# State-space set-up queued behind the weight parts, and four set-up steps per feature tile in the opening

## The chip, the cores and the metric

One core of a Trainium2 chip runs one launch. The metric is the device time of that launch in microseconds; the median over three runs is compared.

## The reference

Two layers of a hybrid encoder trunk on 256 tokens of width 1024, in float32. Cut to what matters here:

```
for l in range(2):
    sh1, sc1, g1, ... g3 = split(silu(c) @ mod_w[l] + mod_b[l], 9)
    h = rms_norm(x, ffn1_norm[l]) * (1 + sc1) + sh1
    x = x + 0.5 * g1 * ((silu(h @ w_gate) * (h @ w_up)) @ w_down)     # first FFN, inner width 2816
    h = rms_norm(x, mix_norm[l]) * (1 + sc2) + sh2
    x = x + g2 * (concat(norm(attention), norm(s5_mixer), norm(conv)) @ w_out)
    h = rms_norm(x, ffn2_norm[l]) * (1 + sc3) + sh3
    x = x + 0.5 * g3 * swiglu(h)                                       # second FFN
return rms_norm(x, final_norm)
```

The `s5_mixer` is a diagonal state-space model with 16 groups of 64 complex states. Before any token is seen, it needs numbers that depend on the parameters alone: `exp(dt*a)` and its powers, the input matrices times these powers, the output matrices times them, and so on. This is the set-up of which the change speaks. The convolution's weights are laid out in it as well.

## The kernel before

**Weights.** All weights come as units of 128 x 1024 float32 (0.5 MB) through one stream (`Stream`, lines 63 to 128). A unit is loaded by the sync queue (SP) into one of six raw buffers. A weight unit is then prepared: ScalarE rounds it to `hi` (line 100), VectorE takes the rest `lo = raw - hi` (line 102), and TensorE multiplies with both (lines 328 to 330). There are six `hi` and six `lo` buffers. A raw buffer is given back when its `lo` is done. Between the weight units lie modulation units: VectorE itself multiplies and sums them (`macc`, line 365, two operations per unit), and the buffer is given back after that. `done` (line 126) counts a used weight unit and prepares further ones, up to five ahead.

**First FFN of layer 0.** It has an opening (`start`, line 484) for the first three of eleven column blocks. Eight feature tiles go through it; for each the scale and shift are first summed out of `mod_w` (`mod_cols`, for two tiles at a time, called for the next pair at the odd tiles), which ends for each tile in `hfs` on ScalarE (line 520) and `xTl` on VectorE (line 522). Then the tile's weights are prepared (`weights`) and 18 products run. At the end of each tile two set-up steps are traced, queued behind the newest `xTl` and `hfs`. After the opening, `silu` and `h` (lines 757 and 759) and two transposes (line 768) follow for its three blocks. The eight other blocks have four gate/up units each (`gt`, line 721) and the down units behind (`down`, line 775), 54 weight units in all, with 48 modulation units mixed in.

**Set-up.** `ssm_small` (line 825) and `ssm_layer` (line 962) are Python generators; each `yield` ends a step. For layer 0 a generator chains `setup_cols2`, `ssm_small(0)` and `ssm_layer(0)`, 59 steps; for layer 1 the last two, 58 steps. `ssm_small` works on tiles of 16 to 128 columns. In `ssm_layer`, lines 1011 to 1019 build `W` and `O` with products (lines 1014 and 1016) and sums (line 1018) of 512 columns, lines 1028 to 1040 the powers `Ec` and `Es`, lines 1057 to 1091 `R`, the kernel `Km`, the convolution's `W4` and `Tp`. A hook (`stages`, line 1497) traces steps at ticks: one tick follows each gate/up unit and each down block. `SLOTS0 = (1, 37, 43)` spreads 43 steps over 37 ticks from tick 1 of layer 0's first FFN, `SLOTS1 = (1, 42, 58)` the 58 of layer 1 over 42 ticks of layer 0's second FFN. Steps left over are traced after the last tick.

**Order.** Every engine runs a fixed queue. A planner writes the queues before the launch: among the instructions that are ready by its own estimate it takes the one that was traced first, with some blocks raised in rank (`high_priority`). So a set-up operation whose inputs are there may be placed ahead of the weight part traced next to it. `issue_after(ins)` ties the instructions traced in its block, on the engine of `ins` alone, to a place behind `ins` in that queue; it adds no wait. `behind` (line 76) does so for several instructions. The steps at the ticks are in no such block.

Of the kernel before, what the change touches and what calls it, by code (L numbers as in the profile page):

```python
# [9 lines left out]
F32 = mybir.dt.float32  # L10
# [3 lines left out]
AF = mybir.ActivationFunctionType  # L14
# [12 lines left out]
ADG = (((0,),(1,),(2,3)),((0,1,2,3),))  # L27
HIP = 150
HIPT = 50
SLOTS0 = (1, 37, 43)  # L30
SSTART = 2
SLOTS1 = (1, 42, 58)
UW = 264
NEG_INADM = -3.0e38
NEG_TAKEN = -3.3e38
# [27 lines left out]
class Stream:  # L63


    def __init__(self, tc, raw_p, hl_p):
        self.tc, self.nc, self.raw_p, self.hl_p = tc, tc.nc, raw_p, hl_p
        self.after_hi = self.after_lo = ()
        self.units = []
        self.loaded = self.prepped = self.got = 0  # L70
        self.used = self.wprep = 0
        self.ready = []
        self.names = []
        self.hb = HB

    def behind(self, ins):
# [13 lines left out]
    def prep_one(self):  # L90
        nc = self.nc
        self.load_upto(self.prepped + RB)
        u = self.units[self.prepped]
        raw = u["raw"]
        if u["kind"] == "w":
            n = u["n"]
            hi = self.hl_p.tile([P, UN], F32R, tag="hi", name="hi")
            lo = self.hl_p.tile([P, UN], F32R, tag="lo", name="lo")
            with self.behind(self.after_hi):
                nc.scalar.activation(hi[:, :n], raw[:, :n], AF.Copy)  # L100
            with self.behind(self.after_lo):
                nc.vector.tensor_sub(lo[:, :n], raw[:, :n], hi[:, :n].bitcast(F32))  # L102
            self.ready.append((hi, lo))
            self.names.append(u.get("name"))
            self.wprep += 1
        else:
            with self.behind(self.after_lo):
                u["use"](raw)
        self.prepped += 1
        self.load_upto(self.prepped + RB)  # L110
# [21 lines left out]
def kernel(  # L132
# [8 lines left out]
    nc = tc.nc  # L141
# [25 lines left out]
    def b8(shape, nm):  # L167
        return two_p.tile(shape, F32, tag="b8", name=nm, bufs=2)
# [171 lines left out]
    st = Stream(tc, raw_p, hl_p)  # L340
# [64 lines left out]
    def unspill(l, m):  # L405

        r = rows[(l, m)] = row_p.tile([P, D], F32, tag="g", name=f"row{l}_{m}")
        nc.gpsimd.dma_start(r, spill[(l, m)][0].partition_broadcast(P))
# [75 lines left out]
    def start():  # L484
# [56 lines left out]
        for k in range(KD):  # L541
# [16 lines left out]
            with st.behind([xti[max(xti)], hfi[max(xti)]]):  # L558
                for _ in range(SSTART):
                    next(setup0, None)  # L560
# [534 lines left out]
    def mixer(l, finish):  # L1095
# [295 lines left out]
        def conv_thread():  # L1391
            for j in range(2):
# [4 lines left out]
                if j == 0:  # L1397
                    U4 = b8([P, 4, 2, UW], "U4")
                for a in range(4):
                    (nc.scalar if a % 2 else nc.gpsimd).dma_start(U4[32 * a:32 * a + 32, :, j], uT[:, j, 8 * a:8 * a + UW])  # L1400
                yield
# [91 lines left out]
    def chain(*gens):  # L1493
        for g_ in gens:
            yield from g_

    def stages(gen, first, n, steps):

        def hook(u):
            if first <= u < first + n:  # L1500
                i = u - first
                for _ in range((i + 1) * steps // n - i * steps // n):
                    next(gen, None)
            elif u >= first + n:
                for _ in gen:
                    pass
        return hook
# [21 lines left out]
    for l in range(L):  # L1529
        if l == 0:  # L1530
            h1 = stages(setup0, *SLOTS0)
        else:
# [16 lines left out]
        mixer(l, after_mix)  # L1549
        ffn(l, 6, after_ffn2, stages(chain(ssm_small(l + 1), ssm_layer(l + 1)), *SLOTS1) if l + 1 < L else None, lambda: unspill(l, 8))  # L1550

# [30 lines left out]
```

## Time and profile before

| what | value |
| --- | --- |
| median of three runs | 1156.27 us (1149.23 to 1161.38) |
| profiled execution | 1159.37 us, its span 1157.5 us |
| TensorE busy | 1082.1 us (93%) |
| VectorE busy | 881.8 us (76%) |
| ScalarE busy | 557.9 us (48%) |
| GpSimd busy | 93.2 us (8%) |
| loads and stores | 251.43 MB, mean 217 GB/s |
| `hi`, line 100 | 314 operations, 328.0 us, 1054 ns each |
| `lo`, line 102 | 314 operations, 379.1 us, 1214 ns each |
| `macc`, line 365 | 224 operations, 166.3 us, 749 ns each |

The span runs from the first to the last instruction of one profiled execution; the device time has a little around it. Busy time is the time in which an engine had an instruction of its own running; matmul ends are modelled, so a busy TensorE need not be at its peak. The granted clock is the share of 2.4 GHz that TensorE's clock had. The DMA share is the busy time of 16 DMA engines as a share of the stretch. In a timeline a bracket gives the idle time ahead of an instruction and what ended it.

### The profile page before, as it was taken

The page shows a single profiled execution, that of the slowest core. Times are in us where ns is not written, and L with a number is a line of the kernel's source. Part 1 is how long each engine was busy: PE and PEld are TensorE (multiplying, and loading weights), DVE is VectorE, ACT ScalarE, POOL GpSimd, SP SyncE. Part 2 cuts the span into 40 slices and gives each one's busy share as a digit, 9 for nine tenths or more (in the row PEclk, how much of TensorE's full clock was granted, in tenths as well). Part 3 has the DMA queues.
Part 4 walks back from the last instruction along what each step waited for, and adds up shares of the span by engine and source line. Part 5 has one row for each costly group of instructions (what it writes and reads, how often), then busy time and mean ns, then how long its engine had stood idle before and what let it go on. Part 6 is the DMA issues. An engine that isn't in the chain of part 4 may idle for free.

```text
span 1157.5 us, 19306 instructions
## 1 busy us (share of the span) xinstructions
PE 1082.1 (93%) x7043; PEld 936.8 (81%) x7043; DVE 881.8 (76%) x1791; ACT 557.9 (48%) x979; POOL 93.2 (8%) x176
## 2 busy tenths in 40 slices
PE   5999978998999999999998999999899998999996
PEld 3578867886886878888996799999698687999996
DVE  4479998888597687899856889889678777665655
ACT  4354433446436565563534534444464656444442
POOL 6000101021012000000020000100100000000000
PEclk9899999989797899999999999999999899999998
DMA  9889788996653139768873799999665234767651
GB/s 254 268 268 304 227 258 287 328 292 175 159 149 78 57 103 301 246 223 287 262 220 108 250 323 360 339 317 328 184 165 148 73 91 146 256 210 221 210 160 55
DMA packets 182671, 251.43 MB, mean 217 GB/s; under 512 B 20023, under 2 KB 132865, under 8 KB 182577
## 3 DMA queue, kind: packets, MB, share of 16 engines
q1 hardware_dynamic: 173728, 240.56, 65.3%
q0 software_dynamic: 5792, 7.52, 2.8%
q10 hardware_dynamic: 3056, 2.13, 0.9%
q8 instruction: 55, 0.90, 0.3%
q14 instruction: 40, 0.32, 0.1%
HBM read 245.19 MB, written 1.11 MB: 213 GB/s over the span
## 4 chain that ended last, share of the span: by engine, by line
PE 56%; DMA 7%; DVE 6%; ACT 3%; issue 2%; SPq 1%; ACTq 0%; DVEq 0%
PE ps_gt L328 7%; PE ps_gt L329 7%; PE ps_gt L330 7%; PE ps_y L330 5%; PE ps_y L328 5%; PE ps_y L329 5%; DMA raw<-in_mod_w_dram 3%; DMA raw<-in_ffn_w_gu_dram 2%; DVE lo L102 2%; DVE macc L365 2%; ACT hi L100 1%; PE ps_idx L1201 1%; PE ps_gu L328 1%; PE ps_gu L330 1%; PE ps_cv L1408 1%
## 5 line engine op out<-in xcount | busy, mean ns | idle before, releaser
L100 ACT ACTIVATE hi<-raw 128x1024 fp32r<-128x1024 f32 (+1 forms) x314 | 328.0, 1054 | 315.0 <-DMA raw<-in_ffn_w_gu_dram 105.5
L102 DVE TENSOR_TENSOR lo<-raw,hi 128x1024 fp32r<-128x1024 f32 (+1 forms) x314 | 379.1, 1214 | 121.6 <-ACT hi L100 117.6
L328 PE MATMUL ps_gt<-xTh,hi 128*128 128x256 f32 x1120 | 320.2, 288 | 10.4 <-DVE h L745 6.6
L330 PE MATMUL ps_gt<-xTh,lo 128*128 128x256 f32 x1120 | 314.8, 285 | 4.4 <-DVE lo L102 4.4
L329 PE MATMUL ps_gt<-xTl,hi 128*128 128x256 f32 x1120 | 317.7, 285 | 0.0
L328 PEld LDWEIGHTS ps_gt<-xTh,hi 128*128 128x128 f32 x1120 | 216.2, 193 | 17.4 <-DVE h L745 7.6
L330 PEld LDWEIGHTS ps_gt<-xTh,lo 128*128 128x128 f32 x1120 | 214.4, 193 | 6.2 <-DVE lo L102 5.7
L329 PEld LDWEIGHTS ps_gt<-xTl,hi 128*128 128x128 f32 x1120 | 216.7, 193 | 1.8 <-issue 0.8
L365 DVE SCALAR_TENSOR_TENSOR macc<-raw,cond,macc 128x512 f32<-128x512 f32 x224 | 166.3, 749 | 25.8 <-DMA raw<-in_mod_w_dram 24.3
L329 PE MATMUL ps_y<-lo,hTh 128*128 128x512 f32 x352 | 139.9, 397 | 1.5 <-DVE lo L102 1.5
L330 PE MATMUL ps_y<-hi,hTl 128*128 128x512 f32 x352 | 139.5, 396 | 1.0 <-DVE hTl L749 1.0
L328 PE MATMUL ps_y<-hi,hTh 128*128 128x512 f32 x352 | 133.6, 396 | 4.9 <-ACT hi L100 4.5
L397 POOL DMA_DIRECT2D spill<-mrow x64 | 31.3, 496 | 642.0 <-ACT mrow L394 640.5
L328 PEld LDWEIGHTS ps_y<-hi,hTh 128*128 128x128 f32 x352 | 66.0, 189 | 19.3 <-ACT hi L100 5.3
L330 PEld LDWEIGHTS ps_y<-hi,hTl 128*128 128x128 f32 x352 | 67.1, 191 | 17.1 <-DVE hTl L749 2.1
L329 PEld LDWEIGHTS ps_y<-lo,hTh 128*128 128x128 f32 x352 | 67.3, 191 | 16.3 <-DVE lo L102 3.6
L328 PE MATMUL ps_gu<-hi,xTh 128*128 128x512 f32 x96 | 39.8, 415 | 6.8 <-DVE xTh L324 6.8
L743 ACT ACTIVATE silu<-ps_gt 128x256 f32<-128x256 f32 x70 | 25.3, 378 | 40.8 <-PE ps_gt L330 40.7
L330 PE MATMUL ps_gu<-hi,xTl 128*128 128x512 f32 x96 | 39.7, 414 | 3.0 <-DVE xTl L325 3.0
L329 PE MATMUL ps_gu<-lo,xTh 128*128 128x512 f32 x96 | 38.6, 402 | 0.0
L745 DVE TENSOR_TENSOR h<-silu,ps_gt 128x256 f32<-128x256 f32 x70 | 28.0, 417 | 10.6 <-ACT silu L743 10.4
L748 ACT ACTIVATE hTh<-h 128x256 fp32r<-128x256 f32 x70 | 27.4, 410 | 16.6 <-DVE h L745 15.5
(386 smaller groups left out, 1591.5 us busy)
## 6 DMA issues: line engine op xcount, KB each, us to landing
raw<-in_ffn_w_gu_dram SPq DMA_DIRECT2D x140, 512.0 KB
raw<-in_mod_w_dram SPq DMA_DIRECT2D x128, 512.0 KB
raw<-in_ffn_w_down_dram SPq DMA_DIRECT2D x88, 512.0 KB
raw<-in_ffn_w_gu_dram SPq DMA_DIRECT2D x72, 256.0 KB
raw<-in_w_in_dram SPq DMA_DIRECT2D x20, 512.0 KB
raw<-in_mod_w_dram SPq DMA_DIRECT2D x32, 256.0 KB
raw<-in_w_out_dram SPq DMA_DIRECT2D x16, 512.0 KB
row<-spill POOLq DMA_DIRECT2D x6, 512.0 KB, 4.9
```

Source lines behind the costliest of these rows:

```text
L100: nc.scalar.activation(hi[:, :n], raw[:, :n], AF.Copy)
L102: nc.vector.tensor_sub(lo[:, :n], raw[:, :n], hi[:, :n].bitcast(F32))
L328: return [nc.tensor.matmul(ps, xh, wh, start=start, stop=False), nc.tensor.matmul(ps, xh, wl, start=False, stop=False), nc.tensor.matmul(p ...
L329: nc.tensor.matmul(ps, xh, wl, start=False, stop=False),
L330: nc.tensor.matmul(ps, xl, wh, start=False, stop=stop)]
L365: nc.vector.scalar_tensor_tensor(acc, raw[:, 512 * i:512 * i + 512], cond[:, k:k + 1], prev, op0=ALU.mult, op1=ALU.add)
L397: nc.gpsimd.dma_start(d[:, 256 * q:256 * q + 256], r[32 * q:32 * q + 1, 0:256])
L743: nc.scalar.activation(s, ps[i][:, :256], AF.Silu)
L745: nc.vector.tensor_mul(h, s, ps[i][:, 256:])
L748: nc.scalar.activation(hi, h, AF.Copy)
L1201: nc.tensor.matmul(ps[:, nk * i:nk * i + nk], qiT[32 * b:32 * b + 32, 256 * i + P * t:256 * i + P * t + P], kiT[32 * b:32 * b + 32, :nk], ...
L1408: nc.tensor.matmul(pc[32 * q:32 * q + 32, 256 * ct:256 * ct + 256], SS["W4"][:, 32 * ct + 8 * q + b, :], U4[:, q, ct, b:b + 256], start=(b ...
```

## The change

A weight unit's two preparing instructions are kept in a list. At each tick, in both FFNs that carry set-up, the steps are traced in a block that queues their ScalarE and VectorE instructions behind the `hi` and `lo` of the third-newest weight unit traced so far (two back from the newest). In the opening four steps are traced per feature tile, not two, 32 in all, and 27 are left for the ticks.

```
-SLOTS0 = (1, 37, 43)
-SSTART = 2
+SLOTS0 = (1, 37, 27)
+SSTART = 4
 SLOTS1 = (1, 42, 58)
+AHEAD = 2
...
+        self.parts = []
...
             with self.behind(self.after_hi):
-                nc.scalar.activation(hi[:, :n], raw[:, :n], AF.Copy)
+                ih = nc.scalar.activation(hi[:, :n], raw[:, :n], AF.Copy)
             with self.behind(self.after_lo):
-                nc.vector.tensor_sub(lo[:, :n], raw[:, :n], hi[:, :n].bitcast(F32))
+                il = nc.vector.tensor_sub(lo[:, :n], raw[:, :n], hi[:, :n].bitcast(F32))
+            self.parts.append((ih, il))
...
             if first <= u < first + n:
                 i = u - first
-                for _ in range((i + 1) * steps // n - i * steps // n):
-                    next(gen, None)
+
+                with st.behind(st.parts[-1 - AHEAD]):
+                    for _ in range((i + 1) * steps // n - i * steps // n):
+                        next(gen, None)
```

## Rows read from the trace of the kernel before

**Rows 1.** Busy time by stretch: length, busy us (count) per engine, TensorE clock, DMA share, GB/s.

```profile
80.00:120.00 40.00, 39.56 (x269) 36.09 (x270) 36.26 (x80) 20.17 (x37) 2.11 (x3) 1.00 0.91 306
120.00:200.00 80.00, 68.34 (x445) 59.43 (x444) 72.46 (x129) 28.90 (x49) 8.66 (x17) 0.96 0.79 254
200.00:260.00 60.00, 56.56 (x390) 50.95 (x390) 50.43 (x67) 23.79 (x35) 9.07 (x17) 0.94 0.96 312
...
720.00:760.00 40.00, 40.00 (x296) 36.83 (x295) 33.85 (x44) 16.80 (x24) 4.74 (x9) 1.00 1.00 342
```

**Rows 2.** The same view at 5 us, first FFN of layer 0.

```profile
120.00:125.00 5.00, 5.00 (x33) 4.55 (x33) 5.00 (x9) 4.50 (x13) 2.51 (x5) 1.00 0.23 51
...
165.00:170.00 5.00, 1.89 (x5) 0.96 (x4) 5.00 (x10) 1.78 (x3) 0.00 (x0) 0.80 0.91 290
170.00:175.00 5.00, 3.81 (x11) 3.22 (x12) 5.00 (x10) 1.54 (x2) 0.00 (x0) 0.52 0.92 312
```

**Rows 3.** VectorE in order of time: start us, us, operation, [idle before <- releaser].

```profile
116.60 2.49 DVE L1014 TENSOR_TENSOR W<-bri,sp_cA 128x512 f32<-128x512 f32 x4
119.01 0.74 DVE L365 SCALAR_TENSOR_TENSOR macc<-raw,cond,bias 128x512 f32<-128x512 f32 x1
119.67 1.89 DVE L1016 TENSOR_TENSOR wtmp<-bri,sp_cB 128x512 f32<-128x512 f32 x3
...
122.95 2.49 DVE L1014 TENSOR_TENSOR sl_O<-CRI,sp_oA 128x512 f32<-128x512 f32 x4
...
126.22 1.89 DVE L1018 TENSOR_TENSOR W<-W,wtmp 128x512 f32<-128x512 f32 x3
```

**Rows 4.** Sync queue in order of time, weight-load issues around that stretch.

```profile
116.71 0.37 SPq L429 DMA_DIRECT2D raw<-in_ffn_w_gu_dram  x1
...
126.34 0.37 SPq L429 DMA_DIRECT2D raw<-in_ffn_w_gu_dram  x1
```

**Rows 5.** ScalarE in order of time, the same stretch.

```profile
120.16 0.84 ACT L967 ACTIVATE CmDd<-CRI 64x256 f32<-64x256 f32 x2
...
130.76 1.06 ACT L100 ACTIVATE hi<-raw 128x1024 fp32r<-128x1024 f32 x1 [5.08 <-DMA raw<-in_ffn_w_gu_dram]
```

**Rows 6.** VectorE in order of time, second FFN of layer 0.

```profile
506.08 1.89 DVE L1014 TENSOR_TENSOR W<-bri,sp_cA 128x512 f32<-128x512 f32 x3
```

**Rows 7.** Busy time by stretch, second FFN of layer 0.

```profile
515.00:520.00 5.00, 4.26 (x19) 3.19 (x17) 5.00 (x10) 3.86 (x6) 0.00 (x0) 1.00 0.31 109
520.00:525.00 5.00, 1.81 (x8) 1.81 (x9) 5.00 (x8) 1.14 (x3) 0.00 (x0) 0.80 0.64 202
```

**Rows 8.** Waits from 430 to 640 us: total us, times, longest.

```profile
PE ps_gt L328 <- DVE h L745: 4.9, 2, 3.9
```

**Rows 9.** VectorE in order of time, opening.

```profile
52.30 0.22 DVE L516 SCALAR_TENSOR_TENSOR mcol<-ps_col,mb,ncol 128x1 f32<-128x1 f32 x1 [7.91 <-PE ps_col L514]
...
56.22 0.43 DVE L522 TENSOR_TENSOR xTl<-hfs,xTh 128x256 fp32r<-128x256 f32 x1
56.56 0.17 DVE L886 TENSOR_TENSOR sp_tmp<-sp_tmp 128x16 f32<-128x16 f32 x1
56.65 0.17 DVE L887 TENSOR_TENSOR sp_tmp<-sp_tmp 128x16 f32<-128x16 f32 x1
...
66.84 1.23 DVE L102 TENSOR_TENSOR lo<-raw,hi 128x1024 fp32r<-128x1024 f32 x1 [4.57 <-ACT hi L100]
...
71.07 0.42 DVE L522 TENSOR_TENSOR xTl<-hfs,xTh 128x256 fp32r<-128x256 f32 x1
...
72.00 1.22 DVE L102 TENSOR_TENSOR lo<-raw,hi 128x1024 fp32r<-128x1024 f32 x1
...
79.96 0.75 DVE L759 TENSOR_TENSOR h<-silu,ps_gs 128x256 f32<-128x256 f32 x2
```

**Rows 10.** GpSimd in order of time, opening.

```profile
25.66 0.57 POOL L988 DMA_DIRECT2D dKm<-in_ssm_d_dram  x1 [1.89 <-PE ps_n L236]
```

**Rows 11.** TensorE in order of time, end of the opening.

```profile
80.44 0.44 PE L768 MATMUL ps_hT<-ident,h 128*128 128x128 f32 x2 [1.54 <-DVE h L759]
```

## The prediction

> **What bounds the kernel now.** I read the chain of waits first: it runs along TensorE for most of the span, so a stage can only be shortened where TensorE sits idle or runs at a reduced clock. Second, the busy time of each engine by stretch [rows 1]. From 80 to 120 us TensorE is busy 39.56 of 40 us. From 120 to 200 us it is busy 68.34 of 80, so 11.7 us are lost; from 200 to 260 us 56.56 of 60, 3.4 us more. The granted clock there is 0.96 and 0.94 of the full 2.4 GHz, which is worth another 68.34 x 0.04 + 56.56 x 0.06 = 6.1 us. VectorE is busy 72.46 of the 80 us and the transfers have a share of 0.79, while 1.00 of share goes with 342 GB/s (last row). So everything is nearly full, and something takes turns at being empty.
>
> Third, the same at 5 us [rows 2]: the transfers fall to 0.23 at 120 us and TensorE to 1.89 of 5 at 165 us, with clocks of 0.80 and 0.52. What happens just ahead of that hole is in VectorE's timeline [rows 3]: from 116.60 us to the end of the row at 126.22 it runs four `W` products, three `wtmp`, four `sl_O` and three sums, fourteen operations of 512 columns. Four take 119.01 - 116.60 = 2.41 us start to next start, 0.60 each, 8.4 us for the fourteen. They are state-space set-up, which only the mixer after this FFN uses. Meanwhile the `lo` parts wait, and a raw buffer is given back only by its `lo` (or by `macc`): the sync queue issues a weight unit at 116.71 and the next at 126.34 [rows 4], and ScalarE's `hi` of it sits 5.08 us waiting for that load [rows 5]. TensorE feels it some units later. That is one cause, a burst, and three engines that pay.
>
> The second FFN of layer 0 shows it again while the set-up of layer 1 runs: `W` products from 506.08 us [rows 6], then TensorE busy 4.26 and 1.81 of 5 us [rows 7], with 4.9 us of waiting for `h` on VectorE, 3.9 in one piece [rows 8].
>
> **The change, part by part.** The set-up is a generator of 59 steps. By my count of the yields: 1 to 20 are small (16 to 64 columns), 21 issues loads, 23 is transposes and copies, 24 to 31 build `W` (8 products, 4 sums), 32 to 39 build `O` (the same), 40 to 44 `Ec`/`Es`, 48 to 59 `R`, `K`, `W4`, `Tp`.
>
> *Four steps per tile in the opening.* Steps 17 to 32 move from ticks 1 and later to the opening, and 3 to 16 move to earlier tiles. Each group still stands behind the newest `xTl`/`hfs`. Tiles 1 and 2 stand behind the `xTl` of tile 3; tiles 3 and 4 behind that of tile 5, at 56.22 us; tiles 5 to 7 behind that of tile 7, at 71.07 us [rows 9]. So steps 5 to 12 fall into the 7.91 us that VectorE idles before 52.30, and 13 to 20 begin at 56.5 and reach into the 4.57 us before 66.84. Steps 7 to 12 have 38 operations there, 13 to 20 have 36; at 0.09 us (56.56 to 56.65) that is 3.4 and 3.2 us, at a dependent pace of about 0.2 us 7.6 and 7.2. They cost nothing under that idle; if the planner's order there leaves the idle unused, up to 3 us of `lo` slip at 67 us, which goes to the range.
>
> Steps 21 to 32 are the catch: they are tied to tile 7 and start at 71.07, not earlier. Step 21's nine loads on GpSimd's queue already issue in the opening (the last at 25.66 us [rows 10]), so they don't move. Step 23 has four transposes on TensorE (0.22 us each by the pair at 80.44 [rows 11], 0.9 us) and on ScalarE two copies of `CRI` and two `CmDd` (0.42 each [rows 5], 1.6 us in all); ScalarE has room. Steps 24 to 32 are fourteen operations of 512 columns, 8.4 us of VectorE. Eight of them (24 to 28) are traced ahead of the `lo` of tile 7, which ran at 72.00 and would start near 71.4 + 4.8 = 76.2; six come ahead of the `lo` parts of the first units after the opening. About 20 small operations (2 us) leave that stretch, so VectorE is 6.4 us behind at 80 us. TensorE waits 1.54 us there for the opening's `h` already [rows 11], and `h` (79.96) is traced after those `lo` parts. The price is between 0 (the planner lets `h` through) and 6.4 us; less than nothing is excluded, since nothing in the opening waits for set-up. I take 3.5: `h` is last in line, but a wait there also lets the loads catch up.
>
> *27 steps, not 43, over 37 ticks.* In the FFN remain ten `O` operations, `Ec`, `R`, `K`, `W4`. VectorE's work after 71 us falls only by steps 11 to 18, 48 small operations, about 5 us.
>
> *Steps behind the parts two units back.* No instruction is added; in both FFNs a step's ScalarE and VectorE instructions take a place in the queue after the `hi` and `lo` of the third-newest unit, so they can no longer be pulled forward into a burst. In layer 0 that spreads `O` at 27/37 steps a tick. What queues behind a step is the next `lo`; who waits for that is the sync queue's next load and then TensorE. Upper bound of the gain in layer 0: 11.7 us idle and 68.34 x 0.04 = 2.7 us of clock, 14.4; lower bound 0 (the stage is short of VectorE time anyhow). Of the 24 large operations 14 stay one clump, now 45 us earlier, and 10 are spread, so I take half: 7.2 us. The 3.4 us after 200 I leave.
>
> In the second FFN the clump comes apart (58 steps over 42 ticks) with no opening to pay. Idle is 0.74 + 3.19 = 3.9 us, clock 1.81 x 0.2 = 0.4; bounds 0 and 4.3; VectorE is less loaded there, so I take 3.0. TensorE's transposes of `W` are placed by the planner after the later `W`; the mixer that uses them is far off, so I cost that at nothing; if a transpose is placed too early TensorE waits up to one step, 1.2 us.
>
> Sum: 3.5 - 7.2 - 3.0 = -6.7 us. The profiled execution took 1159.4 us, its span of 1157.5 and 1.9 around it; 1159.4 - 6.7 = 1152.7. It stands 3.1 us over the median of the runs, so against that median I forecast 1150.
>
> **Rivals.** *A, the burst only moves to the opening* (slower). Place: VectorE from 71.07. Price: the full 6.4 us at the first transposes of `h`, and some 2 us of slow matmuls after it, as after the hole at 165 us [rows 2]; nothing comes back, because VectorE has nearly the same work left. 1159.4 + 8.4 - 3.1 = 1165; with the `lo` slip of 3 us 1168. It decides if `h` of the opening runs after 84 us. For: operations that are traced first go first in the timeline at 71 us. Against: the loads keep landing meanwhile. The Trainium skill (TensorE: Matmul & The Clock Gate, section "HAM oscillation — how this bites in real kernels") says that waits for data let the array fall back to half clock, so that each is paid twice; the 0.52 agrees. Chance 0.22.
>
> *B, the loads are the bound.* 54 weight and 48 modulation units of 0.524 MB are 53.5 MB; at 342 GB/s [rows 1] 156 us of the 188 that the stage takes. If what TensorE waits for is bandwidth, spreading the set-up gives nothing in layer 0 and only the second FFN's 3.0 comes: 1153. Against: 0.79 from 120 to 200 is not a full queue. The Trainium skill (DMA: Bandwidth & Descriptors, section "Where 436 GB/s comes from") puts loads from HBM at about 358 GB/s a core; by that the stage's loads would take an estimated 149 us. The trace's 342 is just under it. Chance 0.18.
>
> *C, the burst was all of it.* All 14.4 and 4.3 us come back and the opening hides its part: 1159.4 - 18.7 - 3.1 = 1138. For: before the burst TensorE had no waits (39.56 of 40). Chance 0.22.
>
> *D, nothing changes*: the planner fills the same gaps in another order; 1156. Chance 0.08.
>
> **How the numbers follow.** My forecast has 0.30 (its own range 1144 to 1156). The range runs from C to A, 1138 to 1165. A measurement of this kernel tells about 1% from no change, 1144.7 and 1167.8. Below: C's 0.22 and 0.07 of mine, 0.29. Above: half of A, 0.11. Between: 0.60.
>
> **What would show it.** Right: fourteen `W`/`wtmp`/`sl_O` operations on VectorE between 71 and 85 us; no run of more than two such operations between two `lo` parts after 90 us and around 506 us; the 0.23 of transfers at 120 us and 0.31 at 515 us gone; TensorE above 74 of 80 us from 120 to 200; the 3.9 us wait for `h` gone. Wrong: the first `ps_gt` matmul later than 84 us (A); TensorE's idle from 120 to 200 as before with transfers above 0.9 (B); `W` products still in a row at 506 us (D).

## The result, and the profile after

The changed kernel took 1157.93 us (median of 20 executions, 1151.73 to 1173.16), the kernel before 1156.05 (median of 20, 1143.39 to 1171.19). The ratio is 1.006, with an interval (95%) of 1.0034 to 1.0085; it leaves out executions more than 1.5% above the fastest of their kernel, 7 of the 20 from before (its fastest was 1143.39) and one from after, and `e1`, `e2`, `f2` and `h1` below were profiled in such an execution, so that their stages are set aside. The medians of all executions stand at 1.0016. Either way the change gains nothing, where I forecast 6 us less; by the ratio it costs 0.3 to 0.9%.

The profiled execution took 1156.45 us (span 1154.6), 3 us *less* than that of before, though the medians stand the other way: one execution tells where time goes, not which kernel is faster. Stages are steadier than whole runs. I use the start of the first `ytmp` as the end of the first FFN of layer 0: 264.6 us in the profile of before, 264.1 in that of a kernel with the same first FFN; 269.7 after, 270.1 in a near copy (`f4` below). A third pair with the same first FFN (`g1` and `h3`) is 2.0 us apart, so a difference of 2 us between two stage ends is not read.

Busy time by stretch of the changed kernel, columns as in [rows 1]:

```profile
80.00:120.00 40.00, 35.82 (x214) 32.53 (x214) 34.42 (x52) 15.36 (x24) 0.00 (x0) 0.91 0.78 254
120.00:200.00 80.00, 74.30 (x499) 65.66 (x500) 67.23 (x120) 29.10 (x45) 9.26 (x17) 0.96 0.87 286
200.00:260.00 60.00, 55.84 (x385) 49.94 (x383) 49.77 (x66) 24.76 (x40) 9.11 (x17) 0.94 0.87 291
120.00:125.00 5.00, 4.10 (x37) 3.72 (x38) 3.96 (x6) 1.33 (x2) 0.94 (x2) 1.00 0.92 278
165.00:170.00 5.00, 3.49 (x15) 2.56 (x15) 3.74 (x9) 1.06 (x1) 0.00 (x0) 1.00 0.91 290
170.00:175.00 5.00, 4.53 (x13) 2.82 (x13) 5.00 (x9) 2.25 (x4) 0.00 (x0) 0.66 0.76 226
...
515.00:520.00 5.00, 3.94 (x22) 3.13 (x21) 5.00 (x8) 2.19 (x3) 0.00 (x0) 1.00 0.65 208
520.00:525.00 5.00, 5.00 (x44) 5.00 (x44) 5.00 (x9) 1.72 (x3) 0.00 (x0) 1.00 0.73 220
```

The dip of the transfers at 120 us in [rows 2] is gone (0.23 to 0.92), and TensorE is busy 74.30 of the 80 us from 120 on, where [rows 1] had 68.34. But from 80 to 120 it now has 35.82, where it had 39.56, and from 200 to 260 it has 55.84, where it had 56.56. Added up, from 80 to 260 us TensorE was busy 164.5 us and is now busy 166.0: its idle time moved.

VectorE in order of time at the end of the opening, against [rows 9]:

```profile
67.67 0.42 DVE L525 TENSOR_TENSOR xTl<-hfs,xTh 128x256 fp32r<-128x256 f32 x1
68.00 0.69 DVE L1017 TENSOR_TENSOR W<-bri,sp_cA 128x512 f32<-128x512 f32 x1
...
72.82 0.69 DVE L1017 TENSOR_TENSOR sl_O<-CRI,sp_oA 128x512 f32<-128x512 f32 x1
73.42 1.22 DVE L104 TENSOR_TENSOR lo<-raw,hi 128x1024 fp32r<-128x1024 f32 x1
...
83.25 0.75 DVE L762 TENSOR_TENSOR h<-silu,ps_gs 128x256 f32<-128x256 f32 x2
```

Nine products stand between the last `xTl` and the last tile's `lo`, which starts 5.75 us after `xTl` (0.93 before); the first `h` follows 15.6 us after it (8.9 before). TensorE waits for both, in order of time:

```profile
74.70 0.53 PE L332 MATMUL ps_gs<-lo,xTh 128*128 128x512 f32 x1 [2.63 <-DVE lo L104]
...
83.72 0.69 PE L771 MATMUL ps_hT<-ident,h 128*128 128x128 f32 x2 [5.50 <-DVE h L762]
84.06 0.56 PE L331 MATMUL ps_gt<-xTh,hi 128*128 128x256 f32 x1
```

In [rows 11] that wait for `h` was 1.54 us. Around the two waits the granted clock falls, where the kernel before has 1.00 in the same three stretches:

```profile
75.00:80.00 5.00, 3.22 (x8) 1.97 (x6) 5.00 (x7) 2.21 (x4) 0.00 (x0) 0.66 0.71 193
80.00:85.00 5.00, 1.28 (x6) 1.28 (x7) 5.00 (x7) 0.94 (x3) 0.00 (x0) 0.69 0.93 335
85.00:90.00 5.00, 5.00 (x30) 5.00 (x29) 4.93 (x11) 1.25 (x4) 0.00 (x0) 0.63 0.72 231
```

In the second FFN the clumps of eight and seven products and sums between two `lo` parts come apart into groups of one to four (VectorE, against [rows 6]), and the wait for `h` of [rows 8] falls from 4.9 us to 2.2, its longest piece from 3.9 to 1.1:

```profile
508.77 1.22 DVE L104 TENSOR_TENSOR lo<-raw,hi 128x1024 fp32r<-128x1024 f32 x1
509.90 1.28 DVE L1017 TENSOR_TENSOR W<-bri,sp_cA 128x512 f32<-128x512 f32 x2
511.11 1.28 DVE L1019 TENSOR_TENSOR wtmp<-bri,sp_cB 128x512 f32<-128x512 f32 x2
512.31 1.22 DVE L104 TENSOR_TENSOR lo<-raw,hi 128x1024 fp32r<-128x1024 f32 x1
```

```profile
PE ps_gt L331 <- DVE h L748: 2.2, 3, 1.1
```

So most of what I had drawn of the order came true: in the first FFN no more than two of the large operations stand between two `lo` parts after 90 us. In the second FFN it did not quite: the lines above show four between two `lo` parts, and three follow at 519.89 us, where I had said two at most. The time did not follow in either case.

### The profile page after: what moved, and what is told of

It is laid out like the page before. It is cut to its first block, busy times and chain, and to the rows that moved or that the text cites. A ratio compares the mean times of both kernels' runs of the same rounds, so it can differ in the third digit from the quotient of the medians.

```text
span 1154.6 us, 19288 instructions
## 1 busy us (share of the span) xinstructions
PE 1083.6 (94%) x7043; PEld 934.5 (81%) x7043; DVE 881.7 (76%) x1791; ACT 558.6 (48%) x979; POOL 94.6 (8%) x176
## 4 chain that ended last, share of the span: by engine, by line
PE 59%; DMA 18%; DVE 14%; issue 5%; ACT 4%; SPq 0%; ACTq 0%; POOL 0%; DVEq 0%; POOLq 0%
PE ps_gt L331 7%; PE ps_gt L332 7%; PE ps_gt L333 7%; DMA raw<-in_mod_w_dram 7%; DMA raw<-in_ffn_w_gu_dram 6%; DVE lo L104 5%; PE ps_y L333 5%; PE ps_y L331 5%; PE ps_y L332 5%; DVE macc L368 3%; ACT hi L102 2%; DMA raw<-in_ffn_w_down_dram 2%; PE ps_gu L333 1%; PE ps_gu L331 1%; PE ps_gu L332 1%
## 5 line engine op out<-in xcount | busy, mean ns | idle before, releaser
L332 PE MATMUL ps_y<-lo,hTh 128*128 128x512 f32 x352 | 142.6, 405 | 2.3 <-DVE lo L104 2.3
L331 PE MATMUL ps_y<-hi,hTh 128*128 128x512 f32 x352 | 137.9, 400 | 6.1 <-ACT hi L102 5.7
```

The source lines that it names most:

```text
L331: return [nc.tensor.matmul(ps, xh, wh, start=start, stop=False), nc.tensor.matmul(ps, xh, wl, start=False, stop=False), nc.tensor.matmul(p ...
L332: nc.tensor.matmul(ps, xh, wl, start=False, stop=False),
```

## The experiments

All times are medians, with the ratio to the kernel before in runs on the same chip and its interval. "Queued" means that the steps at the ticks stand behind the parts two units back.

**Taking the change apart.** First the opening alone:

```
-                with st.behind(st.parts[-1 - AHEAD]):
+                with st.behind(()):
```

> Four steps per tile in the opening and 27 for the ticks, steps at the ticks traced as before (no queueing behind parts). Theory (the opening pays, the queueing gives): nine 512-column products still stand ahead of the last lo of the opening, the first h comes about 15 us after the last xTl (8.9 us before, 15.6 with the whole change), and with nothing given back the time is 1156 + 7 = 1163 us; the burst of W products in the second FFN and its 3.9 us wait for h are there again. Rival (the queueing is what costs, the opening is hidden by the rest of the stage): 1156 or below, clearly under the changed kernel's 1158.

1160.6 us, 1.0018 (0.998 to 1.0056), between what the theory (1163) and the rival (1156 or below) wanted. No sign of a gain from leaving the queueing out, but the interval excludes little. Then the queueing alone, in both FFNs:

```
-SLOTS0 = (1, 37, 27)
-SSTART = 4
+SLOTS0 = (1, 37, 43)
+SSTART = 2
```

> Two steps per tile in the opening as before, 43 for the ticks, steps at the ticks queued behind the parts two units back. Theory (the opening pays, the queueing gives): first h about 9 us after the last xTl, no burst of 512-column operations in either FFN, time 1156 - 5 = 1151 us. Rival (the queueing costs: set-up put in the lo queue one by one delays lo as much as the burst did): 1158 us or more, with TensorE in 80 to 200 us of the span no busier than before the change (107.9 of 120 us).

1157.8 us, 1.0033 (0.9991 to 1.0076). My theory wanted 1151, the rival 1158. The same with the queueing in the second FFN only:

```
+                with st.behind(st.parts[-1 - AHEAD] if first + n > 40 else ()):
```

> Kernel before, with only the steps in the second FFN of layer 0 (set-up of layer 1) queued behind the parts two units back. Theory: the 3.9 us wait for h goes and TensorE is above 78 of 80 us from 480 to 560 us of the span (75.1 before, 77.8 with the whole change); time 1156 - 3 = 1153 us. Rival (the burst there is covered by the lead of the weight units and is made up in the same stage): 1156 us, with the wait moved to the end of that FFN.

1154.55 us, 0.9983 (0.9943 to 1.0022), and TensorE busy 79.92 of the 80 us from 480 to 560. The run alone doesn't settle 2 us; the stage does better. From the first `ytmp` after the mixer to the first `ytmp` after the second FFN, the eight kernels that queue there (the changed one among them, and without the four set aside above) take 206.0 to 209.6 us, mean 207.6. Of the five that don't (six buffers), four take 210.1 to 213.2 and one, `g4`, 206.3, mean 211.0. The two pairs that differ in this alone are further apart: 212.6 and 206.0 (before and `e3`), 212.6 and 206.2 (`h3` and `g1`). So a gain there is likely, of 3 to 7 us by the stage and of 2 by the run; that `g4` is as short with the clumps in place says that they are not all that sets this length.

**Is it the products ahead of `h`?** Twenty small steps in the opening, no products:

```
+SLOTS0 = (1, 37, 39)
+SSTART = (4, 4, 4, 4, 4, 0, 0, 0)
```

> The changed kernel, but the opening traces four steps at each of its first five tiles and none at the last three: 20 small steps, so the W and O products (24 on) are all left for 39 steps at the ticks. Theory (nine large products ahead of the last lo and of h are what the opening pays): first h 8 to 10 us after the last xTl, last lo within 2 us of it, time 1149 to 1152 us, 6 to 8 under the changed kernel. Rival (the opening's price is not the products but the fact that VectorE is full from 70 to 200 us, so the same work costs the same wherever it stands): within 2 us of the changed kernel's 1158.

1162.4 us, 1.0062 (1.0026 to 1.0099): my theory is wrong here. The first `h` did come early, at 73.77 us, 7.3 after the last `xTl` at 66.46, and the kernel was no faster for it. All W and O products now stood queued in the first FFN. (Its profile, of 1156.7 us, shows no place that accounts for a run of 1162; where these 6 us lie in an ordinary run is open. In that profile the first FFN ends at 265.1 us, 1.0 after `e3`, although all 24 large operations are queued.) The other way to the same question, `h` of the opening raised in rank:

```
             for j, ps in enumerate(start()):
-                tr(j, act(ps))
+                with tc.high_priority(offset=HIP):
+                    tr(j, act(ps))
```

> The changed kernel with silu, h, the transposes and hTh/hTl of the opening's three blocks raised in rank as those of the other blocks are (same work, other order). Theory (the opening's wait for h, 5.5 us, is on the path): first h within 11 us of the last xTl instead of 15.6, first ps_gt matmul 3 to 5 us earlier after the last xTl, run 1153 to 1155 us. Rival (the stage is short of VectorE time, so what h gains the lo parts lose): the stage from last xTl to first ytmp within 2 us of 202.0, run 1157 to 1159 us.

1159.5 us, 1.0049 (1.0018 to 1.008). This one tested little: the planner put `h` at 83.80 us all the same, with a TensorE wait of 5.8 us. It served as a near copy of the changed kernel, with the first FFN ending at 270.1.

**What do the products cost?** They are left out for layer 0 in the kernel before and in the changed one:

```
             if l == 0:
                 nc.gpsimd.memset(dst, 1.0)
             for g0 in range(0, G, 4):
                 if l == 0:
                     yield
                     yield
                     continue
```

> The kernel before without the 24 operations of 512 columns that build W and O of layer 0 (GpSimd fills both tiles with ones; layer 1's stay): 24 x 0.60 = 14.4 us of VectorE taken out of the first FFN. Theory V (VectorE's time is what this stage lacks, wherever the products stand): the stage from the last xTl of the opening to its first ytmp shortens from 193.5 us by 7 to 14, the run to 1143 to 1150 us. Rival L (loads and raw buffers set the stage): shortens by less than 3 us, run 1154 to 1157 us.

> The changed kernel without the same 24 operations of layer 0 (both tiles filled with ones by GpSimd). Theory P (all that the change does in the first FFN, it does by where these products stand): from last xTl to first ytmp within 2 us of the kernel before without products; run below it by the second FFN's gain alone, 2 to 5 us, and below the changed kernel's 1158 by 8 us or more. Rival S (the small steps in the opening or the queueing itself cost): that stage 3 us or more longer than in the kernel before without products, run not below it.

Before without products: 1158.4 us, 0.9997 (0.9961 to 1.0033). Its first FFN ends at 258.7 us, 5.9 earlier, and TensorE still idles 13.1 us from 80 to 260, where it idled 15.5. So **the burst that I blamed for 14.4 us of lost time accounts for a small part of it**; neither theory's number: the stage from the last `xTl` shortens by 4.9 us, between the two, and the run is near the rival's 1154 to 1157. The changed kernel without products: 1149.8 us, 0.9947 (0.9906 to 0.9987), 8 us below the changed kernel's median. By the runs the same work costs nothing that shows where the kernel before had it (the interval allows 4 us either way; the stage's end says 5.9) and some 8 us where the change puts it. That is theory P of the second text: with the products gone the change costs nothing in this stage, 189.1 us from the last `xTl` against 188.6, though the first of these comes from a profile set aside above.

**What bounds the first FFN?** Three kernels from the one before: half the bytes of its weight units, half of its modulation sums, five raw buffers.

```
+                src = raw[:, :512].rearrange("p (o n) -> p o n", o=1).to_broadcast([P, 2, 512])
...
-                nc.sync.dma_start(raw, w[l, P * k:P * k + P, :])
+                nc.sync.dma_start(raw[:, :512], w[l, P * k:P * k + P, :512])
```

```
-                    for i in range(2):
+                    for i in range(1 if l == 0 and m < 8 else 2):
```

```
-RB = 6
+RB = 5
```

> The kernel before, but the 54 weight units of the first FFN of layer 0 after its opening load half of their bytes (512 columns), and hi and lo read these twice: VectorE, ScalarE and TensorE have the same work, the transfers 54 x 0.262 MB = 14.2 MB less, 41 us at 342 GB/s. Rival B or L (bandwidth sets the stage): TensorE's idle from 80 to 260 us (15.5 of 180 us before) falls under 5 us and the run to 1146 us or below. Theory V (VectorE sets it, and the loads only wait for the buffers that it gives back): idle stays above 10 us, run 1152 to 1157 us, DMA share of that stretch near 0.55.

> The kernel before with one macc operation in place of two for each of the 48 modulation units of the first FFN of layer 0 (half of those sums is left out; loads stay): 48 x 0.67 = 32 us of VectorE less. Theory V (VectorE is what the stage from 80 to 260 us lacks): its idle of 15.5 us of TensorE falls below 6 us, the stage from the last xTl to the first ytmp shortens by 9 us or more (193.5 to 196.1 before), run 1148 us or less. Rival L (the cycle of buffer, load and parts sets it, whatever VectorE's load): shortens by less than 5 us, run 1153 to 1157 us.

> The kernel before with five raw buffers in place of six, in the whole kernel. Theory L (the cycle of buffer, load, hi, lo sets the stages with modulation units): the first FFN alone becomes 10 us or more longer, TensorE's idle from 80 to 260 us over 25 us, run 1175 us or more. Rival V (VectorE's time sets it, buffers are enough): run within 5 us of before, 1156 to 1161 us.

The stretch from 80 to 260 us of half the bytes, half the sums and five buffers, in that order:

```profile
80.00:260.00 180.00, 163.06 (x1079) 143.96 (x1077) 158.64 (x266) 73.15 (x115) 20.19 (x37) 0.95 0.71 215
```

```profile
80.00:260.00 180.00, 171.80 (x1166) 155.03 (x1166) 144.90 (x265) 82.75 (x141) 24.19 (x45) 0.98 0.92 303
```

```profile
80.00:260.00 180.00, 157.03 (x998) 137.22 (x997) 147.96 (x258) 66.83 (x110) 21.50 (x37) 0.94 0.81 262
```

and the first `ytmp` (first of the two times at the end) in the same order:

```profile
L342 DVE TENSOR_TENSOR ytmp<-ps_y,row x24: 681/692/693, 262.2 to 1155.3; 128x512 f32<-128x512 f32 x24
```

```profile
L336 DVE TENSOR_TENSOR ytmp<-ps_y,row x24: 681/692/692, 240.0 to 1125.5; 128x512 f32<-128x512 f32 x24
```

```profile
L336 DVE TENSOR_TENSOR ytmp<-ps_y,row x24: 680/692/692, 278.7 to 1179.1; 128x512 f32<-128x512 f32 x24
```

With 14 MB less to load the DMA share falls to 0.71 and TensorE idles 16.9 us, as much as before: bandwidth doesn't bound this stage. (The run itself, 1168.1 us, 1.0114 with 1.0068 to 1.0159, was slower; its first FFN was not. In its profile the mixer of layer 1 takes 135.9 us, where before has 126.8; why is open.) With some 32 us of VectorE work less the stage ends 24.6 us earlier, and the run takes 1134.9 us, 0.9848 (0.9797 to 0.9899). With five buffers it ends 14.1 us later, 1183.7 us, 1.0264 (1.0197 to 1.033). Here L was right (10 us or more, 1175 or above) and V, which wanted no change, was wrong: with one buffer less VectorE is busy 147.96 of the 180 us, not 159.16, and everything is later. So **VectorE's `lo` and `macc` work in the round of six raw buffers bounds the first FFN**, and not the sum of VectorE's work by itself: taking out 32 us of sums that a buffer waits for gave 24.6 us, taking out 14.4 us of products that no buffer waits for gave 5.9. My reading of the coupling, argued and not measured by itself: when a load is late VectorE idles, and what it didn't do then it does later while everybody waits for it.

**So what does the queueing do there?** The changed kernel without queueing in the first FFN:

```
+                with st.behind(st.parts[-1 - AHEAD] if first + n > 40 else ()):
```

> The changed kernel with the steps of the first FFN traced as before (the opening's four steps per tile and the second FFN's queueing stay). If the queueing in the first FFN costs by itself, as the kernel with queueing in both FFNs (1157.8) against that in the second alone (1154.5) says: 3 us below the changed kernel, 1155 us, end of the first FFN 2 to 4 us earlier than 269.8. If it gives (the prediction's step): 1160 us or more. If neither: 1157 to 1159 us.

1153.4 us, 0.9989 (0.9948 to 1.003), first FFN done at 264.8 instead of 269.7: the queueing costs 5 us there. VectorE after the opening, changed kernel, shows how:

```profile
92.26 0.75 DVE L368 SCALAR_TENSOR_TENSOR macc<-raw,cond,macc 128x512 f32<-128x512 f32 x1 [2.06 <-DMA raw<-in_mod_w_dram]
...
102.14 0.75 DVE L368 SCALAR_TENSOR_TENSOR macc<-raw,cond,bias 128x512 f32<-128x512 f32 x1 [1.21 <-DMA raw<-in_mod_w_dram]
...
107.27 0.75 DVE L368 SCALAR_TENSOR_TENSOR macc<-raw,cond,macc 128x512 f32<-128x512 f32 x1 [2.25 <-DMA raw<-in_mod_w_dram]
...
113.94 0.68 DVE L1017 TENSOR_TENSOR sl_O<-CRI,sp_oA 128x512 f32<-128x512 f32 x1
114.54 0.68 DVE L1019 TENSOR_TENSOR wtmp<-CRI,sp_oB 128x512 f32<-128x512 f32 x1
```

It idles 5.5 us waiting for loads while set-up work whose inputs are there stands further back in its queue. The kernel without that queueing fills the same stretch with O products, sums and powers, and idles 1.7 us for loads; two of the lines:

```profile
88.04 0.68 DVE L1019 TENSOR_TENSOR wtmp<-CRI,sp_oB 128x512 f32<-128x512 f32 x1
...
90.67 1.27 DVE L1021 TENSOR_TENSOR sl_O<-sl_O,wtmp 128x512 f32<-128x512 f32 x2
```

Busy time from 85 to 115 us (third number after the stretch's length is VectorE), queued and not queued:

```profile
85.00:115.00 30.00, 30.00 (x175) 26.99 (x174) 24.42 (x39) 13.36 (x21) 0.00 (x0) 0.94 0.74 232
```

```profile
85.00:115.00 30.00, 29.50 (x175) 26.80 (x176) 28.34 (x60) 13.13 (x22) 0.00 (x0) 0.93 0.73 238
```

24.42 against 28.34 us: 3.9 us of VectorE's work put off into a stage that is short of it.

**Earlier instead.** If VectorE's idle time is what counts, more of the set-up belongs in the opening, before the modulation units come:

```
+SLOTS0 = (1, 37, 27)
+SSTART = (8, 8, 7, 5, 4, 0, 0, 0)
```

with the second FFN queued (`g1`), with neither (`h3`), with both (`h2`):

> Set-up of the opening traced earlier (8, 8, 7, 5, 4, 0, 0, 0 steps after its eight tiles, 32 in all as in the changed kernel), steps at the ticks of the first FFN as before the change, those of the second FFN queued behind the parts. Theory (what the opening pays is that nine products stand between the last xTl and the last lo and h): the products of W now stand between 52 and 66 us where VectorE waits for loads, first h within 10 us of the last xTl, end of the first FFN by 264 us of the span, run 1148 to 1152 us and so below the kernel with the second FFN's queueing alone (1154.5). Rival (the products cost the same anywhere, because VectorE is what the first 260 us lack): end of the first FFN at 266 to 270 us, run 1154 to 1158 us.

> Set-up traced early in the opening (8, 8, 7, 5, 4, 0, 0, 0 steps), no step queued behind parts in either FFN. Theory (VectorE's idle time in the opening is where the products are nearly free; the second FFN's queueing gives its own 2 to 5 us): end of the first FFN near 260 us of the span as with queueing in the second FFN, that second FFN 212 to 213 us long again, run 1153 to 1156 us, 2 to 4 below before. Rival (the early kernel's gain was the second FFN's alone): run 1156 us or above, end of the first FFN 263 us or later.

> The early kernel (8, 8, 7, 5, 4, 0, 0, 0 steps, second FFN queued) with the 27 steps of the first FFN's ticks queued behind the parts as well. Theory (in the first FFN the queueing keeps products out of VectorE's idle time in the opening and puts them among lo parts that VectorE is short of time for): the second half of O stands between lo parts after 85 us, end of the first FFN 2 to 4 us later than 259.5, run 1155 to 1157 us. Rival (queueing is neutral there): end within 1.5 us, run 1152 to 1154 us.

`g1`: 1153.7 us, 0.9991 (0.9952 to 1.003). `h3`: 1158.8 us, 0.9944 (0.9891 to 0.9996); its median is above that of before (1155.7) and its ratio below 1, so its time settles nothing. `h2`: 1160.2 us, 1.0056 (1.0019 to 1.0093). The ends of their first FFN, in that order:

```profile
L339 DVE TENSOR_TENSOR ytmp<-ps_y,row x24: 680/691/692, 259.5 to 1137.2; 128x512 f32<-128x512 f32 x24
```

```profile
L339 DVE TENSOR_TENSOR ytmp<-ps_y,row x24: 680/692/693, 257.5 to 1142.7; 128x512 f32<-128x512 f32 x24
```

```profile
L339 DVE TENSOR_TENSOR ytmp<-ps_y,row x24: 681/692/693, 265.9 to 1147.1; 128x512 f32<-128x512 f32 x24
```

Without queueing the stage ends 5 to 7 us earlier than in the kernel before, with it 6 to 8 later than that. And yet the early kernel's opening is *late*, and `h` follows 12.1 us after the last `xTl`, where the theory wanted 10 at most. VectorE and then TensorE in `g1`:

```profile
64.37 0.69 DVE L1017 TENSOR_TENSOR W<-bri,sp_cA 128x512 f32<-128x512 f32 x1
...
81.25 0.42 DVE L525 TENSOR_TENSOR xTl<-hfs,xTh 128x256 fp32r<-128x256 f32 x1
```

```profile
120.00:200.00 80.00, 80.00 (x571) 73.61 (x570) 69.62 (x93) 32.50 (x46) 8.81 (x17) 1.00 0.97 330
```

Its last `xTl` comes at 81.25 us, 10 to 14 us later than in before and after (71.07 and 67.67), after a burst of all the `W` products, the sort of burst that I took for the fault. Afterwards TensorE is busy 80.00 of 80 us at full clock. This delay in the opening was made up; VectorE's time in the modulation stretch, in the comparisons above, was not. Two more splits:

```
+SSTART = (6, 6, 6, 5, 5, 4, 0, 0)
```

```
+SLOTS0 = (1, 37, 1)
+SSTART = (8, 8, 8, 8, 8, 8, 6, 4)
```

> As the early kernel, with 6, 6, 6, 5, 5, 4, 0, 0 steps after the tiles (32 again). If the early kernel's 13 us later end of the opening (81 instead of 68 us) cost something: opening ends near 72 us, first FFN by 257 us, run 1149 to 1151 us. If what counts is only that VectorE has the products behind it before the modulation units come: the first FFN ends within 2 us of 259.5, run 1152 to 1155 us. If the products fall between the last xTl and h again: 264 to 270 us, run 1155 to 1158 us.

> As the early kernel, with 58 of the 59 steps in the opening (8, 8, 8, 8, 8, 8, 6, 4). If VectorE's time after the opening is what the first FFN lacks: the remaining set-up (powers, W4, sums, some 8 us of VectorE) leaves the ticks, the first FFN ends 2 to 4 us earlier than 259.5, run 1149 to 1151 us. Rival (the opening is full by then, and what is added there delays the lo parts and h of its end as in the changed kernel): end 262 us or later, run 1155 us or more.

The even split took **1149.8 us, 0.9934 (0.99 to 0.9968), 0.7% below the kernel before**; nearly all steps in the opening took 1153.0, 0.9986 (0.995 to 1.0023), first FFN done at 260.1, which is neither its theory (2 to 4 us before 259.5) nor its rival (262 or later). Why the even split should beat the early kernel isn't shown: their intervals overlap, and it is the lowest of many kernels tried, which its interval doesn't allow for. The best version measured is thus the change's larger share in the opening, evenly and a little earlier, and its queueing in the second FFN only.

Three pairs differ in the first FFN's queueing alone, without and with: 0.9983 and 1.0033 (two steps), 0.9989 and 1.006 (four steps, two chips), 0.9991 and 1.0056 (early, two chips). The intervals overlap in the first pair, barely in the third and not in the second; all three say 0.5 to 0.7%, 6 to 8 us. The filling of load waits is shown for four steps per tile alone. For two steps VectorE has 25.2 us from 85 to 115 us with the queueing and without, and in the early pair 23.39 without it and 29.21 with it, behind last `xTl` parts 8 us apart; the cause of these pairs' differences is open. Nor does the price show at the stage's end each time: `e4`, with everything queued, ended its stage at 265.1, though its ratio (1.0062) is that of the other queued kernels.

## Why the prediction was wrong

**The failed step is "steps behind the parts two units back" in layer 0, put at -7.2 us.** It measured about +5 (264.8 to 269.7 at the stage's end, with four steps per tile in the opening): VectorE waited for loads with set-up work held back behind later parts. I had read the burst of [rows 3], then the gap in the loads [rows 4], then TensorE's hole at 165 us [rows 2] as cause and effect, and took all 14.4 us of loss as the bound of the gain. Without any products 13.1 of 15.5 us of idle remain. Nor was the burst one piece; between the lines of [rows 3] stands a `lo`, which parts it into seven and seven:

```profile
121.47 1.22 DVE L102 TENSOR_TENSOR lo<-raw,hi 128x1024 fp32r<-128x1024 f32 x1
```

The holes that remain go with VectorE's `lo` and `macc` work and the six buffers; of the 159 us that VectorE is busy from 80 to 260 us [rows 1] the products were 14.4. The row that could have warned me was [rows 1]: VectorE busy 72.46 of 80 us. I used it as a side remark ("the stage is short of VectorE time anyhow") and not as a part of the bound, by which spreading the work gives little and VectorE idle that the new order leaves is lost.

**The opening, +3.5.** The picture was right nearly to the count: nine products ahead of the last `lo` (I had said eight), `h` last in line. At the end of the stage little of it is left: 264.8 us with the four steps and no queueing in the first FFN, against 264.6 and 264.1. TensorE's 8.1 us of waits for `lo` and `h` were made up, as the early kernel shows more strongly. The term was too large, about 0.5 us in place of 3.5, which is within the 2 us that stage ends scatter.

**The second FFN, -3.0.** Right in sign, as far as the stage lengths tell, and of about the right size or too small: 3 to 7 us. The clumps came apart and the wait for `h` shrank as I had said. My bound of 4.3 counted only the two 5 us stretches of [rows 7].

**The sum.** 0.5 + 5 - 4 = +1.5 us (4 is a value between 3 and 7), against +1.9 between the medians of all executions. So close a match is partly luck: the sum leaves out the mixers, which the change was not meant to touch and which in the two profiles differ by -7.3 us (layer 0) and +4.1 (layer 1).

**The rivals.** *A* was to show by `h` of the opening or the first `ps_gt` after 84 us: `h` came at 83.25 and `ps_gt` at 84.06, so its picture nearly came true, but not its price (1165), and the place of the loss was another. *B* (bandwidth) falls with half the bytes. *C* (the burst was all of it) falls with no products. *D* holds only for the time. The Trainium skill (TensorE: Matmul & The Clock Gate, "HAM oscillation — how this bites in real kernels") states that waits for data bring TensorE back to half clock. The trace agrees: the granted clock is 0.66, 0.69 and 0.63 around the waits at the end of the opening. This didn't decide anything: the kernel without queueing in the first FFN shows it too (0.53, 0.50 and 0.61 in the same three stretches; 0.50 is 1.2 GHz, the lower of the clock's two levels) and ends its first FFN at 264.8 us. The Trainium skill (DMA: Bandwidth & Descriptors, "Where 436 GB/s comes from") gives the rate at which HBM limits one core, about 358 GB/s. It was no bound in this stage: at half the bytes, 215 GB/s and 0.71 of share, TensorE's idle is the same.

## What to carry to other kernels

Before crediting a hole to the burst ahead of it, take the burst's work out altogether: what remains of the hole can't be won by placing that work better. In this kernel, independent work for the engine that a stage was short of did best ahead of the stage, or where the planner could pull it into waits for loads; the rule that held it back behind later parts cost about what those waits would have covered (3.9 us held back, some 5 lost). The same rule probably gains in another stage of the same kernel, so such rules are worth a switch for each stage.

## What the runs showed that I had not expected

- Executions of one kernel scatter with the mean granted clock: the changed kernel took 1152.95 us at 0.957 and 1173.16 at 0.936, and a line through its 20 executions falls 9 us for each 0.01. Differences of 3 us between whole runs are hardly to be read under that. The profiles show a place of it: in thirteen kernels with the same work there (all but `g5` and the four set aside above) the mixer of layer 1 takes 126.8 to 136.3 us, in the order of its granted clock, 0.95 down to 0.86. Which of the two is the cause isn't shown. The kernel before and `h2`:

```profile
819.50:946.30 126.80, 120.77 (x872) 98.89 (x871) 97.16 (x280) 72.70 (x166) 3.97 (x9) 0.95 0.45 123
809.00:944.80 135.80, 130.48 (x873) 106.41 (x872) 97.18 (x279) 72.84 (x166) 4.70 (x10) 0.86 0.42 116
```

- An opening that ended 10 to 14 us later cost nothing at the end of the first FFN (259.5 us), with the same set-up done earlier.
- Halving the bytes of 54 weight units left TensorE's idle as it was (16.9 us against 15.5).
